# Boundary work in scheduler streams of its own, and a third in place of half of some low parts by transfer, in a two-layer encoder

## Chip, core and metric

The kernel runs on one core of a Trainium2 chip. The metric is the device time of one execution in microseconds (us); the time before is the median of three executions.

## The reference, cut to what matters

```python
D_MODEL, SEQ, DEPTH, CHUNK = 1024, 256, 2, 64
for l in range(DEPTH):
    g = norm_gains[l]
    f1 = swiglu(rmsnorm(x, g[0]), ffn_w_gate[l, 0], ffn_w_up[l, 0], ffn_w_down[l, 0])
    x = x + 0.5 * rmsnorm(f1, g[1])
    m = hybrid_mixer(rmsnorm(x, g[2]), w_in[l], ..., rel_bias[l], w_out_att[l], w_o[l])
    x = x + rmsnorm(m, g[3])
    f2 = swiglu(rmsnorm(x, g[4]), ffn_w_gate[l, 1], ffn_w_up[l, 1], ffn_w_down[l, 1])
    x = x + 0.5 * rmsnorm(f2, g[5])
# rmsnorm(x, g) = x * rsqrt(mean(x*x, -1) + 1e-6) * g
# swiglu(h, wg, wu, wd) = (silu(h @ wg) * (h @ wu)) @ wd
# hybrid_mixer: one projection gives u, q, k, v and two gates; an S5 scan on u, chunk
# attention on q, k, v with a relative bias; both gated, added, and multiplied by w_o
```

The input x has 256 rows of 1024 float32 values, and so has the output.

## The kernel before, in words

x lies on the chip as two tiles of 128 rows (t = 0 and 1). All weights come from memory as 368 chunks of 128x1024 float32, 184 a layer (66 for the first FFN, 52 for the mixer, 66 for the second FFN). A chunk is loaded into a `raw` buffer, of which there are 12, and split in two: `wh` is a rounded copy that ScalarE (ACT) makes, and `wl = raw - wh` the low part. A product of float32 accuracy is then three matmuls on TensorE (PE): high by high, high by low, low by high.

`halves` makes `wl` in one of two ways. Mostly VectorE (DVE) subtracts, in one instruction (line 378). For the chunks whose number within the layer is in the list `ADDED`, ACT copies `wh` with its sign turned into `wl`, and GpSimd (POOL) issues a transfer that adds `raw` to it in memory (`add_to`, line 382). The list names every second chunk from 44 on, eleven in each layer, which are used at the end of the first FFN. The `raw` buffer is held until that transfer has landed.

Six of the twelve FFN blocks of a layer (two in the first FFN, four in the second) are computed with seven products in place of eight, which costs DVE additions on the weights and on the results (`seven`). S5 tables for a layer are prepared ahead of its mixer (`prep`), among the first FFN's work.

An FFN or the mixer ends in `boundary`, once for each row tile: ACT squares the result out of PSUM and sums over rows; DVE multiplies the same banks by gains (`fg`, `fgg`); a tiny DVE instruction (line 405) and a power on POOL (line 393) give the row's scale; DVE adds the scaled result to `pre` (which `pre_gain` has made from x and the next norm's gain, line 378), and PE transposes that sum (line 432) into the left operand of what comes next. Then x itself is brought up to date by two DVE instructions, and `row_scale` squares it on ACT (128x1024) and takes another power for the next norm.

The order of all instructions is made by a list scheduler, `Graph.schedule`. Each operation has a due time, the least over its users of the user's due time less the cost and a latency, and less a margin where the user is of another stream:

```python
            for s in o.succ:
                m = MARGIN.get(o.stream, 0.0) if s.stream != o.stream else 0.0
                d = min(d, s.due - m - o.cost - self.latency(o, s))
```

Among the operations that could start next in the plan, an engine takes the one due first, if buffers are free. An engine then works off its instructions strictly in the order that comes out, so what stands ahead in a queue and waits holds all that is behind it. SyncE's queue (SP) issues the loads, POOL's queue the powers, the adding transfers and small MEMSETs. Loads of the relative bias go through SP into blocks that POOL's MEMSETs (line 359) then clear in part, so such a MEMSET waits for its load.

Of the kernel before, what the change touches and what calls it, by code (L numbers as in the profile page):

```python
# [38 lines left out]
ORDERED = ("blk", "ps", "s1", "s2", "s4", "s16", "gain")  # L39
LAG = 3  # L40
TAU = 1.395
MARGIN = {"conv": 7.558, "conv0": 3.423, "task": 7.748, "att0": 37.576, "s50": 37.749, "att1": 28.585, "sums": 3.0, "s51": 29.753, "prep": 40.0}
PREP_AT = (3, 149)
BIAS_AT = 50
LOOK = 0.027
# [7 lines left out]
DMA_RATE = 350e3  # L53
ADD_LAT = 8.0
BY_DMA = ((3, 4), (3, 4))
ADDED = range(44, 66, 2)


class Buf:
# [79 lines left out]
class Graph:  # L139
# [69 lines left out]
    def schedule(self):  # L209
        for o in reversed(self.ops):  # L210
            d = 1e9
# [3 lines that stand above are left out]
# [109 lines left out]
class Kern:  # L324
# [154 lines left out]
    def weight(self, i):  # L479
        if i not in self.ws:  # L480
# [3 lines left out]
            parts = (slice(0, 512), slice(512, 1024)) if i < 2 else (slice(0, 1024),)  # L484
            self.ws[i] = self.halves(self.load(i, parts), parts, i % LAYER_CHUNKS in ADDED)
            g.stream, g.rank, g.due = keep
# [91 lines left out]
    def pre_gain(self, t, l, i):  # L578
        if l >= DEPTH:
            return None  # L580
        x, g = self.x[t], self.gain(l, i)
        out = []
        for h in range(2):
            s = slice(h * 512, (h + 1) * 512)
            a = self.blk()
            self.tt(a, x[:, s], g[:, s], ALU.mult)
            out.append(a)
        return out

    def boundary(self, t, l, i, banks, scale, eps, nl_, ni_, pre):  # L590
        x, g = self.x[t], self.gain(l, i)
        gg = self.gains(l, i, nl_, ni_) if pre else None
        ss = self.small(2)
        fg, fgg = [self.blk(), self.blk()], [None, None]
        half = [slice(0, 512), slice(512, 1024)]
        for h in range(2):
            junk = self.blk(BF16, 1024)
            self.act(junk[:, :512], banks[h], AF.Square, accum_out=ss[:, h:h + 1], scale=scale)
            if pre:
                fgg[h] = self.blk()  # L600
                self.tt(fgg[h], banks[h], gg[h], ALU.mult)
        for h in range(2):
            self.tt(fg[h], banks[h], g[:, half[h]], ALU.mult)
        rs = self.rsqrt(ss[:, 0:1], ss[:, 1:2], eps)
        xs = None
        if pre:
            for h in range(2):
                self.stt(pre[h], fgg[h], rs, pre[h])
            xs = self.to_lhs(pre)
        for h, a, b in ((0, 0, 512), (1, 0, 512)) if pre else ((0, 0, 512), (1, 0, 384), (1, 384, 512)):  # L610
            c = slice(512 * h + a, 512 * h + b)
            self.stt(x[:, c], fg[h][:, a:b], rs, x[:, c])
            if not pre:
                self.dma(self.out_d[t * P:(t + 1) * P, c], x[:, c])
        return xs, self.row_scale(t) if pre else None

    def sums(self, xs):
        self.mode("sums", "bulk")
# [702 lines left out]
```

## Time and profile before

| | |
|---|---|
| median of three executions | 1142.31 us (1141.41 to 1143.92) |
| profiled execution | 1140.49 us, of which the profile's span is 1138.7 us |
| PE busy | 1116.7 us (98% of the span) |
| DVE busy | 947.4 us (83%) |
| ACT busy | 752.4 us (66%) |
| POOL busy | 96.8 us (9%) |
| loads from memory | 202.96 MB |

The busy time of an engine is the time in which at least one of its instructions runs. PE's is close to the span, so what an edit of the order can give back is in the few places where PE stands idle; what it can cost is a new place of that kind.

### The profile page before, as it was taken

The numbers are of one execution on the slowest core, as the hardware profiler recorded it, in microseconds if no ns is written. First come the engines' busy times: TensorE is split into PE (matmuls) and PEld (weight loads), VectorE is DVE, ScalarE is ACT, GpSimd is POOL, SyncE is SP. The second block draws the span as 40 slices with busy tenths as digits, with TensorE's granted clock in tenths as the row PEclk, the third lists the DMA queues.
The fourth block names the chain that finished last, engine by engine and source line by source line (L and its number), as shares of the span: only waits on it lengthen the run. The fifth ranks groups of instructions, "written<-read, shape, count | busy, mean of one in ns | idle before, by whom it ended". The sixth has DMA issues, their size and how long they took to land.

```text
span 1138.7 us, 15993 instructions
## 1 busy us (share of the span) xinstructions
PE 1116.7 (98%) x5728; PEld 887.3 (78%) x5728; DVE 947.4 (83%) x1396; ACT 752.4 (66%) x1072; POOL 96.8 (9%) x137
## 2 busy tenths in 40 slices
PE   8999999999999999999999999999999999999997
PEld 6778777777778888777888888777777888888886
DVE  6998874796877899999899789567959688999983
ACT  7857685637754687677577567846386456887752
POOL 1101120000000020101020012200000000211000
PEclk9999999999999999999999999999999999999999
DMA  9875997535374566889749679963534655779951
GB/s 348 235 304 136 328 308 218 175 107 186 102 254 167 190 144 201 280 277 265 268 133 277 221 202 319 292 220 132 169 128 145 226 185 166 184 210 280 288 185 37
DMA packets 70351, 241.75 MB, mean 212 GB/s; under 512 B 8192, under 2 KB 8960, under 8 KB 70272
## 3 DMA queue, kind: packets, MB, share of 16 engines
q1 hardware_dynamic: 60192, 204.03, 50.3%
q0 software_dynamic: 10080, 36.70, 17.3%
q8 instruction: 45, 0.74, 0.2%
q14 instruction: 34, 0.28, 0.1%
HBM read 202.96 MB, written 1.05 MB: 179 GB/s over the span
## 4 chain that ended last, share of the span: by engine, by line
PE 74%; DVE 10%; ACT 6%; issue 5%; DMA 5%; POOL 0%; SPq 0%; DVEq 0%; POOLq 0%; ACTq 0%
PE ps L418 69%; DVE wl L378 5%; PE ps L432 3%; DMA raw<-in_wall_dram 3%; ACT blk L371 3%; ACT wh L371 2%; DVE blk L378 2%; DMA wl<-raw 2%; PE ps L424 1%; DVE raw L378 1%; DVE blk L397 1%; ACT raw L371 1%; POOL s L393 0%; SPq L354 0%; ACT L371 0%
## 5 line engine op out<-in xcount | busy, mean ns | idle before, releaser
L418 PE MATMUL ps<-wh,blk 128*128 128x512 f32 x2848 | 879.6, 400 | 5.2 <-DVE blk L378 2.2
L418 PEld LDWEIGHTS ps<-wh,blk 128*128 128x128 f32 x2848 | 530.9, 188 | 131.0 <-ACT blk L371 4.1
L371 ACT ACTIVATE wh<-raw 128x1024 fp32r<-128x1024 f32 (+1 forms) x442 | 454.7, 1052 | 253.3 <-PE ps L418 197.7
L378 DVE TENSOR_TENSOR wl<-raw,wh 128x1024 fp32r<-128x1024 f32 (+1 forms) x420 | 497.8, 1213 | 126.9 <-ACT wh L371 125.2
L418 PE MATMUL ps<-wl,blk 128*128 128x512 f32 x1424 | 525.2, 399 | 1.4 <-DVE wl L378 1.4
L418 PEld LDWEIGHTS ps<-wl,blk 128*128 128x128 f32 x1424 | 266.9, 188 | 63.5 <-DVE wl L378 4.4
L371 ACT ACTIVATE blk<-ps 128x512 fp32r<-128x512 f32 (+4 forms) x156 | 86.0, 562 | 70.7 <-PE ps L432 50.1
L378 DVE TENSOR_TENSOR blk<-ps,blk 128x512 fp32r<-128x512 f32 (+2 forms) x164 | 109.1, 670 | 13.7 <-ACT blk L371 13.4
L432 PE MATMUL ps<-ident,blk 128*128 128x128 f32 x432 | 78.4, 275 | 1.8 <-ACT raw L371 1.8
L382 POOL DMA_DIRECT2D raw<-raw x48 | 41.7, 872 | 340.7 <-ACT raw L371 265.8
L432 PEld LDWEIGHTS ps<-ident,blk 128*128 128x128 f32 x432 | 55.1, 140 | 19.4 <-ACT raw L371 2.7
L371 ACT ACTIVATE blk<-blk 32x128 f32<-32x128 f32 (+4 forms) x148 | 59.0, 399 | 15.9 <-DMA blk<-in_sp_dram 9.1
L393 POOL TENSOR_TENSOR s<-s,mhalf 128x1 f32<-128x1 f32 x24 | 24.2, 1007 | 488.9 <-DVE s L405 488.9
L378 DVE TENSOR_TENSOR raw<-raw,raw 128x1024 f32<-128x1024 f32 x48 | 58.0, 1216 | 0.1
L371 ACT ACTIVATE blk<-ps,s 128x512 f32<-128x512 f32 (+1 forms) x68 | 43.7, 655 | 20.3 <-PE ps L418 13.7
L371 ACT ACTIVATE raw<-raw 128x1024 f32<-128x1024 f32 x48 | 50.2, 1052 | 5.1 <-DVE raw L378 5.1
L378 DVE TENSOR_TENSOR blk<-blk,blk 128x512 f32<-128x512 f32 (+3 forms) x70 | 42.5, 624 | 0.1
L371 ACT ACTIVATE blk<-blk,s 128x128 f32<-128x128 f32 (+2 forms) x76 | 34.6, 485 | 7.5 <-DVE blk L378 7.4
L397 DVE SCALAR_TENSOR_TENSOR blk<-blk,s,blk 128x512 f32<-128x512 f32 x44 | 32.5, 744 | 0.9 <-ACT blk L371 0.8
L382 POOL DMA_DIRECT2D wl<-raw x22 | 19.1, 866 | 108.1 <-ACT wl L371 54.3
L378 DVE TENSOR_TENSOR blk<-ps,raw 128x512 f32<-128x512 f32 x32 | 19.8, 678 | 6.8 <-PE ps L418 6.8
L418 PEld LDWEIGHTS ps<-blk,blk 128*32 128x32 f32 (+2 forms) x256 | 15.4, 147 | 12.0 <-issue 9.8
(100 smaller groups left out, 447.1 us busy)
## 6 DMA issues: line engine op xcount, KB each, us to landing
raw<-in_wall_dram SPq DMA_DIRECT2D x366, 512.0 KB, 5.5
raw<-raw POOLq DMA_DIRECT2D x48, 512.0 KB, 5.7
wl<-raw POOLq DMA_DIRECT2D x22, 512.0 KB, 8.3
gain<-in_gains_dram SPq DMA_DIRECT2D x22, 256.0 KB, 4.4
blk<-in_bias_dram SPq DMA_DIRECT2D x8, 256.0 KB, 5.8
raw<-in_wall_dram SPq DMA_DIRECT2D x4, 256.0 KB, 3.9
blk<-in_sp_dram SPq DMA_DIRECT2D x4, 256.0 KB, 8.5
x<-in_x_dram SPq DMA_DIRECT2D x3, 256.0 KB, 5.3
```

The lines of the kernel that those rows point to most:

```text
L371: self.nc.scalar.activation(out=out.ap(), in_=in_.ap(), func=func, **k)
L378: lambda: self.nc.vector.tensor_tensor(out=out.ap(), in0=a.ap(), in1=b.ap(), op=op))
L382: lambda: self.nc.gpsimd.dma_start(out=out.ap(), in_=in_.ap(), accum_op=ALU.add), func="dma")
L393: lambda: self.nc.gpsimd.tensor_tensor(out=out.ap(), in0=a.ap(), in1=b.ap(), op=ALU.pow))
L397: return self.g.op("dve", cost, [out], [a, s, b], lambda: self.nc.vector.scalar_tensor_tensor(out=out.ap(), in0=a.ap(), scalar=ap(s), in1= ...
L418: return self.g.op("pe", cost, [out], [lhsT, rhs], lambda: self.nc.tensor.matmul(out.ap(), lhsT=lhsT.ap(), rhs=rhs.ap(), start=start, stop ...
L424: self.nc.tensor.matmul(out.ap(), lhsT=lhsT.ap(), rhs=rhs.ap(), start=start, stop=stop)
L432: lambda o=o, s=s: self.nc.tensor.transpose(o.ap(), s.ap(), self.ident.ap()))
```

## The change

Two streams with margins are added. `pre_gain` and the products of gains for the boundary go to the stream "pre" (due 10 us earlier to users of another stream), the rest of a boundary and its `row_scale` to "edge" (4 us earlier), but for the last boundary, which stays in the main stream. And the list `ADDED` names every third chunk from 44 on, eight a layer in place of eleven.

```diff
@@ -39,7 +39,7 @@
 ORDERED = ("blk", "ps", "s1", "s2", "s4", "s16", "gain")
 LAG = 3
 TAU = 1.395
-MARGIN = {"conv": 7.558, "conv0": 3.423, "task": 7.748, "att0": 37.576, "s50": 37.749, "att1": 28.585, "sums": 3.0, "s51": 29.753, "prep": 40.0}
+MARGIN = {"pre": 10.0, "edge": 4.0, "conv": 7.558, "conv0": 3.423, "task": 7.748, "att0": 37.576, "s50": 37.749, "att1": 28.585, "sums": 3.0, "s51": 29.753, "prep": 40.0}
 PREP_AT = (3, 149)
 BIAS_AT = 50
 LOOK = 0.027
@@ -53,7 +53,7 @@
 DMA_RATE = 350e3
 ADD_LAT = 8.0
 BY_DMA = ((3, 4), (3, 4))
-ADDED = range(44, 66, 2)
+ADDED = range(44, 66, 3)
 
 
 class Buf:
@@ -579,17 +579,21 @@
         if l >= DEPTH:
             return None
         x, g = self.x[t], self.gain(l, i)
+        self.mode("pre", "main")
         out = []
         for h in range(2):
             s = slice(h * 512, (h + 1) * 512)
             a = self.blk()
             self.tt(a, x[:, s], g[:, s], ALU.mult)
             out.append(a)
+        self.mode()
         return out
 
     def boundary(self, t, l, i, banks, scale, eps, nl_, ni_, pre):
         x, g = self.x[t], self.gain(l, i)
+        self.mode("pre", "main")
         gg = self.gains(l, i, nl_, ni_) if pre else None
+        self.mode("edge" if pre else "main", "main")
         ss = self.small(2)
         fg, fgg = [self.blk(), self.blk()], [None, None]
         half = [slice(0, 512), slice(512, 1024)]
@@ -612,7 +616,9 @@
             self.stt(x[:, c], fg[h][:, a:b], rs, x[:, c])
             if not pre:
                 self.dma(self.out_d[t * P:(t + 1) * P, c], x[:, c])
-        return xs, self.row_scale(t) if pre else None
+        rs = self.row_scale(t) if pre else None
+        self.mode()
+        return xs, rs
 
     def sums(self, xs):
         self.mode("sums", "bulk")
```

The instructions on PE are the same in number, and in the same order up to about a tenth of the program; behind that the order of every engine changes. On DVE three subtractions a layer are added; from ACT three copies a layer and from POOL three adding transfers a layer are taken.

Three places follow, with the numbers that tell buffers of one kind apart. The first is PE in the second row tile's attention, in the first layer (the second layer's reads alike). `ps_557` and `ps_550` get transposed softmax weights, which ACT copies out to `blk_551` and `blk_558`, and L424 is the product with the values; `ps_562`, `ps_790` and `ps_576` are products with weights. Before:

```order
L418 MATMUL ps_562_2551<-wh_573_2525,blk_378_2082 128x512
L432 MATMUL ps_557_2680<-ident_1_63,blk_553_2591 128x128
L418 MATMUL ps_562_2551<-wh_573_2525,blk_378_2082 128x512
L432 MATMUL ps_550_2675<-ident_1_63,blk_546_2583 128x128
L432 MATMUL ps_557_2680<-ident_1_63,blk_553_2591 128x128
L432 MATMUL ps_550_2675<-ident_1_63,blk_546_2583 128x128
L432 MATMUL ps_557_2680<-ident_1_63,blk_553_2591 128x128
L424 MATMUL ps_544_2705<-blk_551_2697,blk_543_2540 64x128
L424 MATMUL ps_544_2705<-blk_558_2701,blk_543_2540 64x128
```

After:

```order
L432 MATMUL ps_557_2693<-ident_1_63,blk_553_2621 128x128
L418 MATMUL ps_562_2568<-wh_573_2534,blk_378_2039 128x512
L418 MATMUL ps_790_2714<-wh_564_2379,blk_394_2142 128x512
L418 MATMUL ps_790_2714<-wl_565_2512,blk_394_2142 128x512
L418 MATMUL ps_790_2714<-wh_564_2379,blk_394_2142 128x512
L418 MATMUL ps_790_2714<-wl_565_2512,blk_394_2142 128x512
L418 MATMUL ps_790_2714<-wh_564_2379,blk_396_2154 128x512 x2
L418 MATMUL ps_576_2729<-wh_578_2580,blk_375_2020 128x512
L424 MATMUL ps_544_2731<-blk_551_2716,blk_543_2554 64x128
L424 MATMUL ps_544_2731<-blk_558_2722,blk_543_2554 64x128
```

Seven weight products (`ps_790` and the first of `ps_576`) have moved in between the last transpose and the product with the values; before, it stood right behind the transposes.

The second place is SP's queue at the end of the first FFN (layer 0; layer 1 alike): `blk_417` to `blk_420` are the four bias loads, `gain_631` a gain's two halves, `raw` weight chunks. Before:

```order
L354 DMA raw_499_1838<-in_wall_dram 128x1024
L354 DMA raw_502_1859<-in_wall_dram 128x1024
L354 DMA blk_417_1882<-in_bias_dram 128x512
L354 DMA blk_418_1890<-in_bias_dram 128x512
L354 DMA blk_419_1897<-in_bias_dram 128x512
L354 DMA blk_420_1904<-in_bias_dram 128x512
L354 DMA raw_505_1911<-in_wall_dram 128x1024
L354 DMA raw_508_1923<-in_wall_dram 128x1024
L354 DMA raw_515_1952<-in_wall_dram 128x1024
L354 DMA raw_518_1971<-in_wall_dram 128x1024
L354 DMA gain_631_1989<-in_gains_dram 128x512 x2
```

After:

```order
L354 DMA raw_499_1795<-in_wall_dram 128x1024
L354 DMA raw_502_1831<-in_wall_dram 128x1024
L354 DMA gain_631_1854<-in_gains_dram 128x512
L354 DMA raw_505_1875<-in_wall_dram 128x1024
L354 DMA gain_631_1854<-in_gains_dram 128x512
L354 DMA raw_508_1916<-in_wall_dram 128x1024
L354 DMA blk_417_1930<-in_bias_dram 128x512
L354 DMA blk_418_1938<-in_bias_dram 128x512
L354 DMA blk_419_1944<-in_bias_dram 128x512
L354 DMA blk_420_1955<-in_bias_dram 128x512
L354 DMA raw_515_1965<-in_wall_dram 128x1024
L354 DMA raw_518_1992<-in_wall_dram 128x1024
```

The bias loads have moved behind both halves of the gain and behind two weight chunks, `raw_505` and `raw_508`; `raw_508` takes the buffer that `raw_464` had. On POOL nothing changes about them: the four MEMSETs on `blk_417` to `blk_420` stand, before and after, directly ahead of the power `s1_374`, the row scale of tile 0 at the boundary of the first FFN, whose sum PE transposes next. Those transposes have moved two places of 128x512 ahead on PE.

The third place is DVE at the boundary of the second tile at the mixer's end (layer 0; the same form recurs at other second-tile boundaries): `s1_825` is the power's result for this boundary, made by POOL from `s1_824`; `s1_718` feeds another power, ahead of it in POOL's queue; `blk_813` is `pre`. Before:

```order
L405 TENSOR_SCALAR s1_718_3851<-s1_717_3835 128x1
L378 TENSOR_TENSOR wl_864_3859<-raw_862_3525,wh_863_3844 128x1024
L378 TENSOR_TENSOR wl_867_3869<-raw_865_3541,wh_866_3854 128x1024
L405 TENSOR_SCALAR s1_824_3882<-s2_817_3865 128x1
L378 TENSOR_TENSOR blk_821_3885<-ps_815_3659,blk_699_3348 128x512
L378 TENSOR_TENSOR blk_823_3894<-ps_816_3663,blk_700_3440 128x512
L397 SCALAR_TENSOR_TENSOR blk_813_3566<-blk_821_3885,s1_825_3888,blk_813_3566 128x512
```

After:

```order
L378 TENSOR_TENSOR blk_821_3837<-ps_815_3656,blk_699_3294 128x512
L378 TENSOR_TENSOR blk_818_3846<-ps_815_3656,gain_631_1854 128x512
L405 TENSOR_SCALAR s1_718_3850<-s1_717_3832 128x1
L378 TENSOR_TENSOR blk_878_3853<-blk_710_3782,blk_712_3795 128x512
L378 TENSOR_TENSOR wl_864_3861<-raw_862_3530,wh_863_3843 128x1024
L405 TENSOR_SCALAR s1_824_3870<-s2_817_3824 128x1
L378 TENSOR_TENSOR blk_823_3873<-ps_816_3660,blk_700_3317 128x512
L378 TENSOR_TENSOR wl_867_3881<-raw_865_3547,wh_866_3864 128x1024
L397 SCALAR_TENSOR_TENSOR blk_813_3425<-blk_821_3837,s1_825_3878,blk_813_3425 128x512
```

The products that read PSUM (`blk_821`, `blk_818`) have moved ahead of the small instructions, and a subtraction with both inputs in SBUF (`wl_867`) has come between `s1_824` and the first use of the power; another addition and a subtraction (`blk_878`, `wl_864`) now stand between `s1_718` and `s1_824`.

## Rows read from the trace of the kernel before

**Rows 1.** The page: the span, and the busy time of each engine.
```profile
span 1138.7 us, 15993 instructions
...
PE 1116.7 (98%) x5728; PEld 887.3 (78%) x5728; DVE 947.4 (83%) x1396; ACT 752.4 (66%) x1072; POOL 96.8 (9%) x137
```

**Rows 2.** Waits of PE: engine, line waited for; us in total, times, longest.
```profile
PE ps L424 <- ACT blk L371: 2.2, 2, 1.1
PE ps L418 <- DVE blk L378: 2.2, 2, 1.4
PE ps L432 <- ACT raw L371: 1.8, 2, 1.1
...
PE ps L418 <- DVE wl L378: 1.4, 4, 0.5
```

**Rows 3.** Windows: us, then busy PE, PEld, DVE, ACT, POOL, PEclk, DMA.
```profile
111.00:170.00 59.00, 57.69 (x254) 46.09 (x253) 48.97 (x128) 45.10 (x65) 10.42 (x15) 1.00 1.03 318
199.00:215.00 16.00, 16.00 (x76) 12.84 (x76) 14.86 (x22) 9.27 (x15) 2.60 (x5) 1.00 0.62 204
...
400.00:505.00 105.00, 102.21 (x454) 81.38 (x453) 101.03 (x110) 81.06 (x94) 13.78 (x16) 1.00 0.75 218
```

**Rows 4.** Timelines of PE and ACT at the attention (start, us, instruction, idle before).
```profile
270.86 1.04 PE L432 MATMUL ps<-ident,blk 128*128 128x128 f32 x4
272.99 1.57 PE L424 MATMUL ps<-blk,blk 128*64 128x128 f32 x16 [1.10 <-ACT blk L371]
...
272.37 1.06 ACT L371 ACTIVATE blk<-ps 128x512 f32<-128x512 f32 x2
```

**Rows 5.** Timelines of PE, ACT and POOL around 174 us.
```profile
174.63 0.76 PE L432 MATMUL ps<-ident,blk 128*128 128x128 f32 x5 [1.11 <-ACT raw L371]
...
173.98 0.60 ACT L371 ACTIVATE raw<-ps 128x512 f32<-128x512 f32 x1 [1.59 <-DMA wl<-raw]
...
165.04 0.87 POOL L382 DMA_DIRECT2D wl<-raw  x1 [5.30 <-ACT wl L371]
```

**Rows 6.** Timelines of SP, POOL, DVE, PE, 182 to 202 us; landings, 100:330.
```profile
182.42 2.00 SPq L354 DMA_DIRECT2D blk<-in_bias_dram  x4
...
188.33 0.20 POOL L359 MEMSET blk<- 64x128 f32 x1 [14.77 <-DMA blk<-in_bias_dram]
...
190.51 0.20 POOL L359 MEMSET blk<- 64x128 f32 x1 [0.54 <-DMA blk<-in_bias_dram]
199.07 0.56 POOL L393 TENSOR_TENSOR s<-s,mhalf 128x1 f32<-128x1 f32 x1 [8.36 <-DVE s L405]
...
190.14 1.23 DVE L378 TENSOR_TENSOR wl<-raw,wh 128x1024 fp32r<-128x1024 f32 x1 [2.50 <-ACT wh L371]
...
200.09 0.74 DVE L397 SCALAR_TENSOR_TENSOR blk<-blk,s,blk 128x512 f32<-128x512 f32 x1
...
201.15 0.40 PE L418 MATMUL ps<-wh,blk 128*128 128x512 f32 x1
201.38 0.60 PE L432 MATMUL ps<-ident,blk 128*128 128x128 f32 x4
...
DMA to landing us min/median/max: 3.4/4.7/12.2
```

**Rows 7.** The powers (min/median/max ns), and one of them beside DVE.
```profile
L393 POOL TENSOR_TENSOR s<-s,mhalf x24: 547/551/3727, 16.0 to 1133.2; 128x1 f32<-128x1 f32 x24
...
406.04 3.14 POOL L393 TENSOR_TENSOR s<-s,mhalf 128x1 f32<-128x1 f32 x1 [7.48 <-DVE s L405]
...
407.55 1.22 DVE L378 TENSOR_TENSOR wl<-raw,wh 128x1024 fp32r<-128x1024 f32 x1
```

**Rows 8.** The page: costliest groups (busy, mean ns, idle before), and one issue.
```profile
L371 ACT ACTIVATE wh<-raw 128x1024 fp32r<-128x1024 f32 (+1 forms) x442 | 454.7, 1052 | 253.3 <-PE ps L418 197.7
L378 DVE TENSOR_TENSOR wl<-raw,wh 128x1024 fp32r<-128x1024 f32 (+1 forms) x420 | 497.8, 1213 | 126.9 <-ACT wh L371 125.2
...
wl<-raw POOLq DMA_DIRECT2D x22, 512.0 KB, 8.3
```

## The prediction

> **What bounds the kernel now.** First the page [rows 1]: PE is busy for 1116.7 us of a span of 1138.7, so 22 us of idling are all that a new order can touch, and part of them are the start and the end, which the change leaves as they are. No other engine is near: DVE stands at 83%, ACT at 66%, POOL at 9%. Then the waits of PE [rows 2], which name what the idling in the middle is: 2.2 us in two waits for ACT at L424 (the attention), 2.2 us in two waits for DVE's additions and 1.4 us in four for its low parts (second FFN), and 1.8 us in two waits of the transposes at L432 for ACT (end of the first FFN). These sum to 7.6 us; it is the whole market for gains, and each item occurs at one place in each layer or less often. Last the windows [rows 3]. At the end of the first FFN PE is busy 57.69 of 59 us; around the boundary behind it, 16.00 of 16, so the boundary that the new margins are laid on has no wait of PE in it. In 400:505 DVE is busy 101.03 of 105 us and PE loses 2.8 us: there DVE is the limit, and an order alone doesn't make it shorter.
>
> **What the shorter list costs.** Each layer gets three more subtractions on DVE of 1213 ns and loses three copies of about 1.05 us on ACT and three transfers that land 8.3 us after issue [rows 8]. The 3.6 us of DVE fall into a stretch where it is busy 48.97 of 59 us [rows 3], so 10 us of idle time cover them; without that cover they would cost 3.6 us a layer. I take nothing for them. What they give is at the slot wait [rows 5]: at 174.63 PE's transposes had waited 1.11 us for ACT, whose copy into `raw` at 173.98 had itself waited 1.59 us for the buffer that an adding transfer, issued at 165.04, held until it landed about 8.9 us later. The second layer has the shorter twin (1.8 less 1.1, so 0.7 us) [rows 2]. In the new order that buffer is again one held by an adding transfer (`raw_344` in place of `raw_338`), issued about as far ahead, but ACT has fewer copies in front of it. The bounds are nothing and all of it, with the extra hand-over some 2.2 us; I take half: **-1.1 us**.
>
> **The attention.** At 270.86 PE runs the last four transposes, and the product at L424 begins at 272.99 after 1.10 us of waiting [rows 4]: ACT copies the transposed weights out from 272.37 on, and PE has nothing else in its queue. The other layer waits the same 1.1 us [rows 2]. The first piece of order shows seven products of 128x512 between the two now. One of those takes 0.23 us of PE (201.15 to 201.38, [rows 6]), so they cover 1.6 us, more than the wait. They can stand there because the second tile's `row_scale` is due earlier, so PSUM banks that wait for it come free earlier. With the restart of the pipeline the two waits are worth up to 1.3 us each; they are worth nothing if ACT, which gets the earlier copies too, is later by as much. I take 1.1 each, near the full end, since the cover is longer than the wait: **-2.2 us**.
>
> **The bias loads.** This is what I fear. In the trace the four loads go out in 2.00 us from 182.42, and the MEMSETs that wait for them start at 188.33 and 190.51 [rows 6]: 5.9 us from issue to MEMSET for the first, and, with the last issued about 184.0, 6.5 for the last. The power on POOL comes at 199.07, long after. In the new order the loads stand behind `raw_508`, whose buffer is free when the subtraction at 190.14 (1.23 us) is over, at 191.4. With about 0.4 us for that issue and 0.5 each for the next, the last bias load goes out about 193.4. Landing after 5.9 to 6.5 us, and with 0.2 us for the MEMSET, the power starts at 199.5 to 200.1 in place of 199.07. From power to transposes the trace shows 0.56 us, DVE's instruction at 200.09 (0.74 us) and some 0.2 us to PE: 1.9 us in all, so transposes at 201.0 if the power isn't held; PE reached them at 201.38, and the new order has them two products earlier, near 200.9. So a landing of L us costs PE about L - 5.4 us, here 0.5 to 1.1, and nothing at or below 5.4; in the stretch 100:330 half of SP's transfers landed within 4.7 us, and the longest took 12.2 [rows 6]. Behind the held power, DVE's queue waits too, but PE's is what counts. I take 0.4 us a layer, between nothing and 0.8: **+0.8 us**.
>
> **The second tile's boundary.** A power takes 551 ns in the median, but the one at 406.04 took 3.14 us [rows 7], while DVE ran additions and subtractions with both inputs in SBUF, the last at 407.55. Before, the instructions behind the boundary's small one read PSUM; now a subtraction of 1.22 us stands there, and two more ahead hold back another power that POOL has to do first (third piece of order). DVE's own subtraction must be over before the first use of the power, so a held power adds at most what is left after it, some 0.65 us; there are three such boundaries, each with 0 to 0.65 us. I take 0.8 in all: **+0.8 us**.
> The Trainium skill speaks of this on its page "SBUF — State Buffer", in the section "Who interferes with whom": a DVE instruction with two inputs in SBUF contends with a GpSimd instruction that reads SBUF, and the loser is blocked entirely. The power at 406.04 agrees with it, though most powers do not show it. By the page's rule each of the three powers would be held to the end of that subtraction, the sum's term would be 1.9 in place of 0.8, and this speaks against the change.
>
> **The second FFN.** DVE fills 400:505 and its additions are used by PE as soon as they are done (2.2 us and 1.4 us of waiting, [rows 2]). The new order puts two additions even closer to their users and moves others away. Bounds: all 3.6 us given back, or as much again added; nothing in the order lightens DVE there, so I take **+0.3 us**.
>
> **Sum.** -1.1 - 2.2 + 0.8 + 0.8 + 0.3 = -1.4 us on the profiled execution's 1140.49. That one stands 1.82 us below the median, 1142.31, of the three; on the median the forecast is 1140.9 us. A measurement of this kernel tells changes of about 0.2% (2.3 us) from none, so the bounds lie at 1140.0 and 1144.6.
>
> **Rivals.** *All gains, no new wait.* Both attention waits (2.6 us) and the slot wait (2.2 us) go, and the late bias loads land in time: -4.8 to -3 us, 1137.5 to 1139.3, faster. For it: the cover is longer than the wait, and the landings are uncertain by more than the margin. Against: the bias loads are late by the trace's own times. Chance 0.23.
> *Gains given back.* The powers at the second tile's boundaries are held to the full 1.9 us, the second FFN loses 1 to 2, and the attention gains only half, since ACT is the late engine there; or the margins buy nothing, since PE did not wait at a boundary [rows 3]. 0 to +2 us, 1142.3 to 1144.3. Chance 0.13, nearly all of it no change. (This is the case that the skill's "SBUF — State Buffer" leads to.)
> *The bias loads decide.* Without its +0.8 us the sum is 1140.1; to pass 1144.6 the two layers must lose 2.25 us each, which L - 5.4 gives at L = 7.6 us. The first layer's slowest was 6.5, so it takes a busier stretch; adding transfers take 8.3 us [rows 8], and 12.2 has been seen [rows 6], but transfers are fewer now. At L = 8 us it is 2.6 a layer, 1145.3. Chance 0.15, slower.
>
> **Chances.** The forecast's own case, -2.6 to -0.2 us (1139.7 to 1142.1), has 0.47, some 0.10 of it beyond the bound for faster; 0.02 are left for a slower time by something not seen. Faster is 0.23 + 0.10 = 0.33, slower 0.15 + 0.01 + 0.02 = 0.18, and 0.49 remain for no change. The range runs from the first rival's full end, 1137.6, to the third's, 1145.4; the ends beyond hold about 2 in 10.
>
> **What would show it.** Right: L424 with no wait, or with products in front of it; transposes near 174 us with half the wait; four MEMSETs at 197 to 200 us and the power directly behind the last, with a short wait of PE's transposes near 201 us; powers of 1 to 3 us at three second-tile boundaries. Wrong: the same L424 wait of 1.1 us (ACT is the limit, not the order); MEMSETs at 202 us or later; or new waits in the second FFN beyond 400 us, which would make it slower with none of these.

## The result, and the profile after

The changed kernel takes 1126.32 us (median of four, 1125.73 to 1127.01); beside it the kernel before took 1141.86 us. The ratio is 0.9862, with a 95% interval of 0.9844 to 0.9881: about 15.5 us faster, where 1.4 us had been forecast and 1137.6 was the low end of the range. The profiled execution took 1127.01 us, with a span of 1125.2 in place of 1138.7, 13.5 us less.

The page after, the span and the busy times, against [rows 1]:

```profile
span 1125.2 us, 15956 instructions
...
PE 1107.9 (98%) x5728; PEld 885.6 (79%) x5728; DVE 954.2 (85%) x1402; ACT 749.1 (67%) x1066; POOL 99.4 (9%) x131
```

Here stands what the prediction missed. PE has the same 5728 instructions, and its *busy* time fell by 8.8 us. The idle time of PE fell by 4.7 us only (22.0 to 17.3). So most of the gain came out of time that was counted as busy.

PE's waits after (us in total, times, longest), against [rows 2]:

```profile
PE ps L418 <- ACT blk L371: 3.9, 5, 1.8
PE ps L418 <- DVE blk L378: 2.3, 1, 2.3
...
PE ps L418 <- DVE wl L378: 0.8, 2, 0.5
PE ps L418 <- DVE blk L403: 0.5, 1, 0.5
```

The two waits at L424 and the two at L432 for ACT's copy into `raw` (the prediction's slot wait) are gone; the waits for DVE in the second FFN have become one, of 2.3 us.

The time hidden in "busy" is in a place that no step of the prediction spoke of. `prep` ends in 32 small products a layer with weights of 128x32 (64 records in the trace), between the stall at 174 us and the boundary. PE's timeline there in the kernel before (start, us, instruction, count), with the end of the attention behind it:

```profile
180.26 0.27 PE L432 MATMUL ps<-ident,blk 128*128 128x128 f32 x1
180.46 0.25 PE L418 MATMUL ps<-blk,blk 128*32 128x32 f32 x2
...
182.25 0.31 PE L418 MATMUL ps<-blk,blk 128*32 128x32 f32 x10
182.49 0.49 PE L418 MATMUL ps<-wh,blk 128*128 128x512 f32 x1
182.91 0.31 PE L418 MATMUL ps<-blk,blk 128*32 128x32 f32 x10
183.15 0.49 PE L418 MATMUL ps<-wl,blk 128*128 128x512 f32 x1
...
185.76 0.26 PE L418 MATMUL ps<-blk,blk 128*32 128x32 f32 x6
185.95 0.50 PE L418 MATMUL ps<-wh,blk 128*128 128x512 f32 x1
...
274.49 1.09 PE L432 MATMUL ps<-ident,blk 128*128 128x128 f32 x8
```

And in the changed kernel:

```profile
175.87 0.60 PE L432 MATMUL ps<-ident,blk 128*128 128x128 f32 x4
176.22 0.48 PE L418 MATMUL ps<-wl,blk 128*128 128x512 f32 x1
176.53 0.40 PE L418 MATMUL ps<-wh,blk 128*128 128x512 f32 x1
...
181.30 0.71 PE L418 MATMUL ps<-wh,blk 128*128 128x512 f32 x2
181.94 0.76 PE L418 MATMUL ps<-blk,blk 128*32 128x32 f32 x64
182.64 0.51 PE L418 MATMUL ps<-wh,blk 128*128 128x512 f32 x1
```

All 64 go in 0.70 us when they go together, 0.011 us each. Before, they went in ten pieces, with transposes and 128x512 products between. No row shows a wait; the starts show the cost. From 182.25 to the next piece at 182.91 there are ten small records and one large product: 0.11 and 0.23 us of work [rows 6] in 0.66 us, so a piece costs 0.32 us more. The whole place, 180.26 to 185.95, is 5.69 us for six large products (1.4 us), five transposes (0.55) and the 64 (0.70): 3.0 us lost. In the second layer it is 5.70 us (742.23 to 747.93), the same loss. From here on, *by the starts* means this reading: the time from one start to a later one, less what the same instructions take where nothing disturbs them.

The attention after, against [rows 4]:

```profile
268.15 0.86 PE L418 MATMUL ps<-wh,blk 128*128 128x512 f32 x3
268.94 1.09 PE L424 MATMUL ps<-blk,blk 128*64 128x128 f32 x16
269.96 0.50 PE L418 MATMUL ps<-wl,blk 128*128 128x512 f32 x1
```

L424 follows without a wait, and its 16 records take 1.02 us (268.94 to 269.96) where before they took 1.50 (272.99 to 274.49): they waited again inside, for ACT's second copy, which ended at 273.42 (the next of them starts at 273.48). Before it, the four transposes at 270.86 are 0.44 us of work, and 1.69 us lay between their end and L424; now 0.10 us lie between the last product and L424. Together 2.07 us a layer.

### The profile page after: what moved, and what is told of

Same layout as the page of the kernel before. It is cut to its first block, busy times and chain, and to the rows that moved or that the text cites. A ratio compares the mean times of both kernels' runs of the same rounds, so it can differ in the third digit from the quotient of the medians.

```text
span 1125.2 us, 15956 instructions
## 1 busy us (share of the span) xinstructions
PE 1107.9 (98%) x5728; PEld 885.6 (79%) x5728; DVE 954.2 (85%) x1402; ACT 749.1 (67%) x1066; POOL 99.4 (9%) x131
## 4 chain that ended last, share of the span: by engine, by line
PE 87%; DVE 5%; issue 2%; ACT 2%; DMA 2%; POOL 1%; SPq 0%; POOLq 0%; DVEq 0%; ACTq 0%
PE ps L418 81%; PE ps L432 4%; DVE wl L378 3%; DMA raw<-in_wall_dram 2%; PE ps L424 1%; DVE blk L378 1%; ACT blk L371 1%; POOL s L393 1%; ACT wh L371 1%; DVE blk L397 1%; DVE raw L378 0%; SPq L354 0%; DVE x L397 0%; DVE s L405 0%; POOLq L1322 0%
## 5 line engine op out<-in xcount | busy, mean ns | idle before, releaser
L378 DVE TENSOR_TENSOR wl<-raw,wh 128x1024 fp32r<-128x1024 f32 (+1 forms) x426 | 505.7, 1215 | 104.3 <-ACT wh L371 103.7
L432 PE MATMUL ps<-ident,blk 128*128 128x128 f32 x432 | 74.7, 273 | 0.0
L393 POOL TENSOR_TENSOR s<-s,mhalf 128x1 f32<-128x1 f32 x24 | 32.1, 1338 | 448.3 <-DVE s L405 448.2
L432 PEld LDWEIGHTS ps<-ident,blk 128*128 128x128 f32 x432 | 54.6, 140 | 15.9 <-PE ps L418 1.3
L397 DVE SCALAR_TENSOR_TENSOR blk<-ps,s,blk 128x512 f32<-128x512 f32 (+1 forms) x24 | 15.8, 658 | 9.7 <-ACT blk L371 9.4
L382 POOL DMA_DIRECT2D wl<-raw x16 | 13.8, 865 | 111.7 <-ACT wl L371 56.3
```

The lines of the kernel that those rows point to most:

```text
L378: lambda: self.nc.vector.tensor_tensor(out=out.ap(), in0=a.ap(), in1=b.ap(), op=op))
L382: lambda: self.nc.gpsimd.dma_start(out=out.ap(), in_=in_.ap(), accum_op=ALU.add), func="dma")
L393: lambda: self.nc.gpsimd.tensor_tensor(out=out.ap(), in0=a.ap(), in1=b.ap(), op=ALU.pow))
L397: return self.g.op("dve", cost, [out], [a, s, b], lambda: self.nc.vector.scalar_tensor_tensor(out=out.ap(), in0=a.ap(), scalar=ap(s), in1= ...
L432: lambda o=o, s=s: self.nc.tensor.transpose(o.ap(), s.ap(), self.ident.ap()))
```

## Experiments

Two causes were to be told apart: **broken-up runs** (time inside busy, at the 128x32 products) and **waits** (L424, L432, the second FFN: what the prediction had counted). In each case the ratio is to the kernel before, from runs on the same chip.

**The 128x32 products gathered, nothing else.** On the order that the scheduler of the kernel before puts out:

```python
small = [o for o in order if o.stream == "prep" and o.eng == "pe" and o.cost == 0.05][32 * l:32 * l + 32]
at = order.index(small[-1])
order[:at + 1] = [o for o in order[:at + 1] if o not in small] + small
```

> The kernel before, with the 32 products of 128x32 of the S5 tables in each layer issued by TensorE in one run in place of ten pieces; nothing else moves. Theory (broken-up runs): each return to a 128x512 product costs about 0.3 us in the trace of before, 18 fewer of them make it 5 to 7 us faster, about 1135.5. Rival (waits): the gain came from waits at L424, L432 and the second FFN, which this kernel keeps; no change, 1141 to 1142.

Measured: 1134.73 us against 1141.11, ratio 0.9945 (0.9928 to 0.9963). Its PE timeline has the 64 records in one piece:

```profile
182.33 0.76 PE L446 MATMUL ps<-blk,blk 128*32 128x32 f32 x64
183.02 0.73 PE L446 MATMUL ps<-wh,blk 128*128 128x512 f32 x2
```

6.4 us from an edit that removes no wait: its waits at L424 are still 2.2 us, those of the transposes for ACT's copy into `raw` 2.5. The rival is out for this part, and the two layers' 6.0 us by the starts agree.

**The changed kernel with them spread again.** The 32 products of each layer in eight pieces of four, one 128x512 product taken from behind them between each two.

> The changed kernel, with the 32 products of 128x32 of each layer issued in eight pieces of four with one 128x512 product between; nothing else moves. Theory (broken-up runs): 14 more returns at 0.3 us each, 4 to 5 us slower than the changed kernel, about 1130.7. Rival (waits): no change against the changed kernel, 1126.3.

Measured: 1134.90 us, ratio 0.9944 (0.9925 to 0.9962), where the change has 0.9862: about 9 us of its gain are lost (8.6 by the medians, 0.0082 by the ratios), twice what was expected; the spans of the profiled executions differ by 6.7. Eight pieces in place of one show the same price:

```profile
182.55 0.27 PE L459 MATMUL ps<-blk,blk 128*32 128x32 f32 x8
182.74 0.50 PE L459 MATMUL ps<-wh,blk 128*128 128x512 f32 x1
183.17 0.27 PE L459 MATMUL ps<-blk,blk 128*32 128x32 f32 x8
...
200.30 0.63 PE L473 MATMUL ps<-ident,blk 128*128 128x128 f32 x4 [1.31 <-DVE blk L438]
```

0.62 us a round for 0.09 and 0.23 us of work, 0.30 lost in each. The second part is the last row: the boundary's transposes wait 1.31 us. POOL's timeline says why:

```profile
198.64 0.20 POOL L400 MEMSET blk<- 64x128 f32 x1 [0.46 <-PE ps L459]
198.81 0.56 POOL L434 TENSOR_TENSOR s<-s,mhalf 128x1 f32<-128x1 f32 x1
```

The power follows the last MEMSET on the bias without a pause. That MEMSET's row names PE, but the bias load it clears, issued at 192.59, landed only at 198.53, just ahead of it. So it is the prediction's rival *The bias loads decide*, at its place and for its reason, in a kernel where it had not been expected. Fourteen pieces at 0.30 us and the waits of these transposes (1.31 us here, 0.37 in the second layer) make 5.9 of the 6.7 us between the spans.

**The shorter list alone.**

```diff
-ADDED = range(44, 66, 2)
+ADDED = range(44, 66, 3)
```

> The shorter list of adding transfers alone, no new streams. Its order has the 128x32 products in three runs a layer (before ten, after the change one), and nothing moved in front of L424. Theory (broken-up runs): 14 fewer at 0.3 us and half to all of the slot wait, 1134.5 to 1136.5. Rival (waits): only the slot wait, 1140 to 1141.

Measured: 1134.56 us, ratio 0.9939 (0.9925 to 0.9952). The waits of PE:

```profile
PE ps L424 <- ACT blk L371: 2.2, 2, 1.1
PE ps L432 <- ACT raw L371: 2.1, 2, 1.5
```

Neither is shorter than before. So the list, which has to do with transfers, gave its 6.5 us by the way: it moved other operations in the plan, and the 128x32 products came to lie in three pieces for ten. Fourteen pieces at 0.3 us are 4.2 us of it, and PE's waits for DVE, the one at L403 left out, are 1.2 us shorter (3.6 before, 2.4 here); the rest isn't placed. The slot wait, for which the prediction had credited it, stayed.

**The streams alone.** The change without the new list.

> The two new streams alone, with the list of before. Its order has the 128x32 products in eight runs a layer, and seven products in front of L424 as the changed kernel has. Theory (broken-up runs): 4 fewer at 0.3 us and about 3 us from the two waits at L424, 1137 to 1138. Rival (waits, the streams carry the gain): 1129 to 1131.

Measured: 1131.71 us, ratio 0.9919 (0.9903 to 0.9935). More than the 3 to 4 us expected and less than the rival's 10 to 12. L424 isn't in its list of waits, and the slot wait is 0.3 us:

```profile
PE ps L432 <- ACT raw L371: 0.3, 1, 0.3
```

The expectation had the attention at 3 us for the two layers (it is 4.1, by the starts), and nothing for the slot wait (1.5) or for the waits for low parts (1.1: 1.4 us before, 0.3 here). With 1.2 us for the four pieces these make 7.9 of the 8.3 us between the spans.

**The streams alone, and the 128x32 products gathered.**

> The two streams with the list of before, and the 128x32 products of each layer issued in one run (eight runs in the streams alone). If the list acts on the time only through the runs, this reaches the changed kernel, 1126 to 1127.5. If the list gives something else (the slot wait, fewer transfers), it stays 1 to 3 us behind, 1128 to 1129.

Measured: 1127.79 us, ratio 0.9882 (0.9866 to 0.9898); the change has 0.9862 (0.9844 to 0.9881). The streams alone stand at 0.9919, so the gather gives 0.0037 of the 0.0057 that the list gives on top of them. By these middle values two thirds of the list's part come through the broken-up runs; the intervals leave room for all of it, and for much less.

**The stream edge alone.** `pre_gain` and the gain products stay in the main stream, list of before.

> The stream edge alone (the rest of the boundary and row_scale, 4 us), pre_gain and the products of gains left in the main stream, list of before. Theory: the moved row_scale is what lets products in front of L424, so it keeps the gain of both streams, 1131 to 1132.5. Rival: the 10 us for pre carries half or more of it, 1136 or above.

Measured: 1135.07 us, ratio 0.9954 (0.9940 to 0.9968): between the two, so neither expectation holds. The L424 waits are gone here too, so the stream edge is what did that. Whether it is its `row_scale`, as the expectation has it, or the rest of the boundary isn't shown: the two were not moved apart. The slot wait is back at 2.2 us, which this expectation had left out.

**The stream pre alone.**

> The stream pre alone (pre_gain and products of gains, 10 us), list of before. In the profiles the wait of the transposes for ACT's copy into raw (slot wait) is 1.8 us before, 2.1 with the list alone, 2.2 with edge alone, 0.3 with both streams. If pre removes it, 1.5 to 2 us faster than before, 1139 to 1139.5; L424 still waits 1.1 us twice. Rival: it takes both streams together, no change, 1141.

Measured: 1140.79 us against 1141.81, ratio 0.9991 (0.9982 to 1.0001). No gain that can be told from none; its slot wait is 3.0 us.

**Edge and the list, without pre.**

> The change without pre: stream edge and the shorter list. One run of 128x32 products a layer and seven products in front of L424, as in the changed kernel. If pre's share is the slot wait alone, 1.5 to 2 us behind the changed kernel, 1127.8 to 1128.3. Rival: nothing is left for pre once the list is short, 1126.3.

Measured: 1126.92 us, ratio 0.9872 (0.9857 to 0.9887), no difference from the change that the intervals can tell. This doesn't show that pre does nothing beside the short list. Here PE waits 0.7 us at the slot wait, where the changed kernel has none; on the other side this profiled execution kept the full clock in the second FFN, where the changed kernel's lost 1.6 us (next experiment). The intervals would allow pre the 1.5 to 2 us of the expectation. The slot wait (1.8 us before; 2.1, 2.2 and 3.0 with each part alone) falls to 0.3 to 0.9 with both streams or with edge and the list, and is gone in the changed kernel. I can't name one part as its cause; pre with the list was not run.

**The second layer's preparation, begun later.** The second FFN of the first layer is where the changed kernel still waits. Its PE timeline:

```profile
465.33 0.50 PE L418 MATMUL ps<-wh,blk 128*128 128x512 f32 x1 [2.26 <-DVE blk L378]
...
467.87 0.63 PE L418 MATMUL ps<-wl,blk 128*128 128x512 f32 x1
468.29 0.63 PE L418 MATMUL ps<-wh,blk 128*128 128x512 f32 x1
...
470.24 0.40 PE L418 MATMUL ps<-wh,blk 128*128 128x512 f32 x1
```

And the window behind it (us, then busy PE, PEld, DVE, ACT, POOL, PEclk, DMA share, GB/s):

```profile
465.00:470.00 5.00, 4.67 (x13) 3.70 (x14) 4.62 (x9) 1.08 (x2) 0.00 (x0) 0.66 0.77 311
```

After a wait of 2.26 us the granted clock is 0.66 in the next five microseconds: products follow one another every 0.43 us (467.87 to 468.29), the pace of the 1.2 GHz level, for some 3 us. ACT had waited there 6.79 us for a chunk to load. Three of the twelve `raw` buffers are held by the second layer's preparation, so:

```diff
-PREP_AT = (3, 149)
+PREP_AT = (3, 165)
```

> The changed kernel with the second layer's preparation of S5 tables begun 16 chunks later (165 for 149). It takes three raw buffers for its length; in the first layer's second FFN the changed kernel waits 2.26 us for an addition of DVE and then runs eight products at half the clock. If the raw buffers taken make the loads late there, some 2 to 4 us are gained, 1122.5 to 1124.5; if DVE alone is the limit, no change, 1126.

Measured: 1122.63 us, ratio 0.9839 (0.9824 to 0.9854). The stretch 400:520 of the changed kernel:

```profile
400.00:520.00 120.00, 117.21 (x514) 93.98 (x514) 115.31 (x125) 93.22 (x106) 16.37 (x20) 0.99 0.79 223
```

and with the later preparation:

```profile
400.00:520.00 120.00, 120.00 (x535) 96.85 (x534) 119.16 (x124) 96.72 (x108) 15.91 (x20) 1.00 0.83 238
```

PE has no gap left, and DVE is busy 119.16 of 120 us: it does more in the same time. That its inputs come sooner fits: ACT's waits for loads in this stretch fall from 9.4 to 1.9 us. Whether the three buffers alone do it, or also the preparation's own small instructions that leave this stretch, was not told apart. This is the fastest version of the study with the next one, 18.4 us below the kernel before.

**Later still**, at chunk 187, in the second layer.

> The changed kernel with that preparation begun only in the second layer's first FFN (187 for 149). By the buffers' theory the first layer's second FFN runs like the second layer's, which has no wait: 3 to 4 us gained, 1122 to 1123.5. By the other no change there, and DVE's work moved into the first FFN may cost up to 2 us, 1126 to 1128.

Measured: 1122.08 us, ratio 0.9843 (0.9822 to 0.9864): the same. The second FFN is as full as above, but one wait of 1.5 us for ACT's copy into `raw` has come back.

**The same edit on the kernel before** (165 for 149, nothing of the change).

> The kernel before with the second layer's preparation begun at chunk 165 for 149, nothing of the change. If the raw buffers that it holds cause the waits for DVE in the first layer's second FFN (2.2 and 1.4 us in the trace of before), 3 to 4 us faster than before, 1137 to 1138. Rival: the gain of this edit needs the new order, 1141.

Measured: 1136.21 us, ratio 0.9949 (0.9935 to 0.9963), 5.6 us faster; in 400:520 its PE is busy 120.00 of 120 us. The edit doesn't need the new order, and gives somewhat more than the waits it removes there; in this stretch ACT's waits for loads, 9.2 us before, are gone. The slot wait fell too, from 1.8 to 0.8 us, with no part of the change in it.

## Why the prediction was wrong

**What bounds the kernel.** This is the step that failed: "22 us of idling are all that a new order can touch" (the section on the profile before says the same). Busy time was taken for work, and the market for gains put at 7.6 us, where 13.5 came. The trace of before had the other number in it: PE's starts around 180 us, where products follow at 0.42 us in place of 0.23 with nothing waited for. The prediction read PE's waits and gaps, and neither view shows what it costs to go from one weight shape to another. The broken-up runs are 6.0 of the 13.5 us by the starts, and 6.4 us when they are removed alone; the sum had no term for them. The Trainium skill has the rule: its page "TensorEngine Tiling (Array Packing)", section "Key Properties", says that a change of the tiling mode drains TensorE. It gives no price. The trace agrees with it: 0.32 us a piece for pieces of 128x32 weights, while transposes, with 128x128 weights, between the same products cost nothing extra: in the changed kernel four of them and the product behind take 0.66 us (175.87 to 176.53), their own 0.44 and 0.23. The trace shows the price and the place, not the drain itself. The change was not aimed at these products; their order fell out of the planner, so this part of the gain is luck.

**The shorter list.** Covered on DVE, as predicted. The credit for the slot wait was wrong: alone it left the wait at 2.1 us, and gave 6.5 us elsewhere.

**The attention.** The mechanism was right, products in front of L424. The term was mis-sized: -1.1 a layer against -2.07 measured. It took the wait that the view lists, and left out the start-up behind it and the second wait inside the group.

**The slot wait.** Half was taken, -1.1; all of it went: 1.8 us by the list of waits, 2.3 by the starts. (Before, two products from 172.81 are 0.46 us of work, and the transposes behind them begin at 174.63, so 1.36 us; 0.99 in the second layer.) The upper bound of 2.2 was the right size. None of the parts alone removes it, and its cause stays open.

**The bias loads.** +0.8 was taken; PE lost nothing. POOL's timeline after, with a later power:

```profile
193.65 0.20 POOL L359 MEMSET blk<- 64x128 f32 x1 [0.54 <-DMA blk<-in_bias_dram]
194.04 0.56 POOL L393 TENSOR_TENSOR s<-s,mhalf 128x1 f32<-128x1 f32 x1 [0.19 <-DVE s L405]
...
396.80 5.47 POOL L393 TENSOR_TENSOR s<-s,mhalf 128x1 f32<-128x1 f32 x1 [6.83 <-DVE s L405]
```

The last MEMSET came 0.39 us ahead of the power, which waited for DVE. In the second layer the power followed it at once (749.62 and 749.85), without a wait of PE. The order was read rightly, and so was the time of issue: the loads went out at 187.12 in a kernel that was by then almost 5 us ahead (transposes at 195.96, before at 201.38 [rows 6], two products of that by the order): 187.12 and 5.0 make 192.1, close to the 191.8 of the working. What was off is the landing: the last load, issued about 188.5, let its MEMSET start at 193.65, 5.1 us later, where 5.9 to 6.5 had been taken and 5.4 was the point from which PE pays. The margin was thin: spread products were enough to make it a wait of 1.31 us.

**The second tile's power.** 0.8 was taken; PE lost nothing. The boundary's own power (389.43) took 0.55 us and the one ahead of it in POOL's queue (387.57) 0.86. The long one is the third, the last row above: 5.47 us. It follows the update of x, so it is the row scale for the next norm. DVE's timeline beside it:

```profile
396.64 0.68 DVE L378 TENSOR_TENSOR blk<-blk,blk 128x512 f32<-128x512 f32 x1
397.24 2.35 DVE L378 TENSOR_TENSOR wl<-raw,wh 128x1024 fp32r<-128x1024 f32 x2
399.52 1.21 DVE L378 TENSOR_TENSOR raw<-raw,raw 128x1024 f32<-128x1024 f32 x1
400.65 1.22 DVE L378 TENSOR_TENSOR wl<-raw,wh 128x1024 fp32r<-128x1024 f32 x1
401.79 0.74 DVE L397 SCALAR_TENSOR_TENSOR blk<-ps,s,blk 128x512 f32<-128x512 f32 x1
```

Five instructions with two inputs in SBUF follow without a pause, and the power ends only after the first one that reads PSUM has begun. The page "SBUF — State Buffer" of the Trainium skill, section "Who interferes with whom", says that the loser is blocked entirely; the row agrees, and adds that it can stay blocked over a whole chain. No wait of PE stands near it: that scale is used later. The step that failed is the attribution: the row at 406.04 [rows 7], on which the term was built, is the same third power of the kernel before, and says nothing of the two that PE's transposes wait for.

**The second FFN.** +0.3 was taken. Its market of 3.6 us was misread: of the four waits for low parts only one, of 0.53 us, is in the second FFN (467.95). Two are at the end of the first (161.63 and 723.91, 0.26 and 0.33 us), and they are gone; the fourth, at 59.18, stays. In the second FFN PE waits 2.8 us after (0.53 and 2.26), where it waited 2.7 (0.53, 0.78 and 1.41), so the waits there neither grew nor shrank. But the one long wait brought the low clock: eight products at 0.43 for 0.23 us, 1.6 us. That side effect was not in the prediction.

**The whole difference.** Taken by the starts of all of PE's instructions, the 13.5 us between the spans come out as 6.0 for the broken-up runs, 4.1 for the attention, 2.3 for the slot wait, 1.1 for the waits for low parts at the end of the first FFN, and 0.7 in many small places of the mixers, less 0.7 lost in the second FFN (its low clock took 1.6, small pauses that are gone gave 0.9 back). Ahead of all that the change moved, the program's start took 0.7 us longer and the wait at L403 0.6 less, which is scatter. The sum had foreseen 1.4 us; of the other 12.1, half are the broken-up runs, and 3 are the two terms that were right in kind and too small (1.9 at the attention, 1.2 at the slot wait). The first rival, all gains and no new wait, is nearest to what came, but the broken-up runs are not in it either.

## What to carry to other kernels

Don't take an engine's busy time for its work: multiply the count of its instructions by the spacing of the same instruction in an undisturbed run, and look where starts are further apart than that with no wait named. On TensorE keep products with narrow weights together (here 0.3 us a piece), and check after any edit of a planner's numbers whether they still are, since an edit aimed elsewhere can make or break such a run. Test an edit's parts alone before crediting them: here the list that changes transfers gained by moving matmuls.

## Not expected of the hardware

A piece of 128x32 products between 128x512 products cost 0.30 to 0.32 us over its own work, with eight records or ten alike, and no wait in the records. A power that takes 0.55 us in most places took 5.47 us beside a chain of five DVE instructions, in each of three places alike. After a wait of 2.26 us TensorE's granted clock was 0.66 in the next five microseconds, some 3 us of them at the 1.2 GHz level. Six kernels of the study have a wait of 2.1 to 2.3 us at that place; in the profiled executions of five the clock fell to that level behind it, and in one, edge and the list with 2.25 us, it stayed at 1.00.
